# Input normalised with time on the partitions and split once, and the filler ahead of the decay products taken away

## The chip, the cores and the metric

The kernel runs on one core of one Trainium2 chip. The metric is the device time of one execution in microseconds (us), and three executions of a kernel give its median. TensorE (PE) does the matrix products, with a separate queue for its weight loads (PEld); VectorE (DVE), ScalarE (ACT) and GpSimd (POOL) do the elementwise work; SyncE (SP) issues most transfers.

## What is computed

One layer of a hybrid decoder for 1024 time steps and a model width of 1024, all in float32:

```python
xn = rms_norm(x, norm_g)                 # x * rsqrt(mean(x*x, -1) + eps) * g
cols = split_columns(xn @ w_in)
y_a = nsa_attention(cols["a_q"], ...) * silu(cols["a_z"])
y_b = swa_sink_attention(cols["b_q"], ...) * silu(cols["b_z"])
y_c = rwkv7_time_mix(cols["c_shift"], ...) * silu(cols["c_z"])
gates = sigmoid(cols["merge"] + b_merge)
mixed = gates_a * (y_a @ proj_a) + gates_b * (y_b @ proj_b) + gates_c * (y_c @ proj_c)
out = rms_norm(x + mixed @ w_out, final_g)
```

The change is in the first line and in the order of a part of `xn @ w_in`.

## The kernel before

The kernel runs as one program in four parts. `trunk` begins with a prologue that loads x, normalises it and keeps it on the chip as two halves of precision, `x_hi` and `x_lo` (x_hi is x rounded to the shorter type fp32r, x_lo the rest), laid out with the model width on the partitions and time along the row. Then come `rwkv` (branch C, in two passes), `attention` (branches A and B) and `finish` (gates, the three output projections, the last product and the last norm).

Every projection of xn is done by `mm3`: for each of the 8 blocks of 128 along the width, three products, hi by hi, hi by lo and lo by hi. A projection to 128 columns takes 48 matmuls of 128x512, 24 for each half of time, and its weights are loaded and split in the same way by `split_w` (ACT rounds, L196; DVE subtracts, L197). The matmuls of these projections are the rows `pj` (L311, L313, L315).

32 projections (8 gates `z0` to `z7` and 24 merge gates) have no user until late. They are the filler: `fill` is a list of tasks, and `fill.run(ns)` writes so many nanoseconds of their matmuls, by a nominal cost of each, at that place of the program. The budgets are constants (`G_0` ahead of the decay products, `G_LORA` behind them, and so on). What the budgets leave is written by `fill.drain()` when attention has been written. A scheduler that works when the program is built then fixes the order of the rows on each engine, and each engine works through its rows in that order. Each filler task ends with a tanh on ACT, for the z gates a product on DVE (`gs`, L358 and L359), and a store.

The prologue reads the transposed input `xT` in two halves of time (`xr`, 8 blocks of 128x512 each). For each block ACT rounds x times `norm_g` (L235), DVE subtracts (L236), and PE begins the first two projections with it, `wa` (the decay features) and `k0`, on the x that is not yet normalised (L240 to L242). ACT squares the block (L244), DVE and POOL add the squares (L249), and PE sums them over the partitions (L254) and spreads the root over them (L263). DVE then scales the two products by it (L268). After that each block is made once more, now normalised: DVE scales it (L271), ACT rounds (L272), DVE subtracts (L273). The projections `z6` and `z7` follow side by side, all 96 matmuls of them, and then `rwkv` begins.

In `rwkv` the path is serial in its first part: `wa` is evacuated (`z`, L424), shifted in time (POOL L433, DVE L434), goes through a tanh (L438) and into the decay products (L460). From these come exponentials, a scan, the sums over heads (`head_sums`, L400 and L401), and with these the tiles AR and BK, whose products are the first matmuls of the chunks (`GM`, L528). Filler matmuls stand between these steps in PE's order.

At the end `finish` loads the branch outputs `y`, scales and splits them (`y_hi` L1208, `y_lo` L1209) and begins with `pp`, the products of branch C, from y6 and y7.

Of the kernel before, what the change touches and what calls it, by code (L numbers as in the profile page):

```python
# [17 lines left out]
P = 128  # L18
# [24 lines left out]
G_0, WP, PSP = 7200, 1, 0  # L43
START = "wa:0-2 x0:0-1 k0:0-2 x0:1-2 wa:2-8 x0:2-3 k0:2-8 x0:3-4 x0:4-6 x0:6-8 x1:0-2 x1:2-4 x1:4-6 x1:6-8"
# [110 lines left out]
def trunk(ctx, tc, a, out):  # L155
# [46 lines left out]

    x_hi = xhp.tile([P, KT, T], F32R, name="x_hi")
# [3 lines left out]
    first = {}  # L207
    pj0_stack = ExitStack()
    pj0 = pj0_stack.enter_context(tc.tile_pool(name="pj0", bufs=1, space=PSUM))
    with tc.tile_pool(name="x0", bufs=1) as x0, tc.tile_pool(name="x0p", bufs=1, space=PSUM) as x0p:  # L210
        names, xrs = ("wa", "k0"), []
        ws = {n: [x0.tile([P, KT * P], F32R, name=f"w{i}{n}") for i in range(2)] for n in names}
        mean = lined(x0, 1, name="mean")
        dve.memset(mean, 1.0 / D)
        ones = x0.tile([P, P], F32, name="ones")
        pool.memset(ones, 1.0)
        act.activation(lined(x0, 1, name="warm"), eps[:, 0:1], AF.Sqrt)
        for step in START.split():
            what, c = step.split(":")
            c0, c1 = [int(i) for i in c.split("-")]  # L220
            if what in names:
                c = slice(c0 * P, c1 * P)
                load_w(x0.tile([P, (c1 - c0) * P], F32, name=f"raw{step}"), a["w"][W_TILES[what]][:, c], ws[what][0][:, c], ws[what][1][:, c])
            else:
                h = int(what[1])
                if c0 == 0:
                    xrs.append(x0.tile([P, KT, NH], F32, name="xr", bufs=2))
                nc.sync.dma_start(xrs[h][:, c0:c1], a["xT"][:, c0:c1, h * NH:(h + 1) * NH])
        for h in range(2):
            ts = slice(h * NH, (h + 1) * NH)  # L230
# [101 lines left out]
    def side_by_side(*pairs):  # L332

        ws = [weights(name) for name, _ in pairs]
        for h in range(2):
# [3 lines left out]
            for _ in range(KT):  # L339
                for gen in gens:  # L340
                    for _ in range(3):
                        yield next(gen)
# [983 lines left out]
```

## Time and profile before

| | us |
|---|---|
| median of 3 runs | 1198.23 (1197.81 to 1201.52) |
| the profiled execution, its own time | 1200.41 |
| its span, from the first to the last instruction | 1198.6 |
| PE busy in it | 1132.8 (95%) |
| mean granted clock of PE | 0.984 |

The span is the part of an execution that the trace shows. PE's granted clock has two levels, 2.4 GHz (1.00 in a row) and 1.2 GHz; a mean between them says what share of a stretch had which.

### The profile page before, as it was taken

To read this page: it belongs to the slowest core of one execution; us is meant where nothing else is said; L and a number is where in the kernel's file an instruction comes from. 1 tells how busy PE (TensorE), PEld (TensorE's weight loads), DVE (VectorE), ACT (ScalarE), POOL (GpSimd) and SP (SyncE) were. 2 spreads that over 40 slices of the span, in tenths; PEclk is the share of its full clock that TensorE was granted. 3 is DMA by queue.
4 is the path that set the end of the run, shared out by engine and by line. 5 is a ranking of instruction groups with operands and counts; after the bars stand their busy time and mean duration, and the time that the engine had idled before them with its cause. 6 is when DMAs were issued, how large, how long until landed. Compare 5 with 4: busy or idle time off the path is not lost.

```text
span 1198.6 us, 18003 instructions
## 1 busy us (share of the span) xinstructions
PE 1132.8 (95%) x6698; PEld 915.0 (76%) x6698; DVE 769.1 (64%) x1449; ACT 555.9 (46%) x1283; POOL 279.4 (23%) x288
## 2 busy tenths in 40 slices
PE   7698999999999989998999999999999995999997
PEld 5566888767887889886878877887788774778886
DVE  7947782479643632268387878746887776887332
ACT  7435332462423532254466666636666663222322
POOL 3110100021000211127123322231323222263222
PEclk9889999999999999999999999999999998999999
DMA  5121224021231222113111111111211137884221
GB/s 194 35 84 62 62 74 118 28 79 58 66 110 46 62 92 91 31 44 92 59 49 60 60 64 52 50 49 62 63 49 54 40 108 242 298 273 145 71 71 54
DMA packets 66456, 101.92 MB, mean 85 GB/s; under 512 B 16832, under 2 KB 27456, under 8 KB 66112
## 3 DMA queue, kind: packets, MB, share of 16 engines
q1 hardware_dynamic: 64160, 96.41, 25.0%
q10 hardware_dynamic: 1440, 2.26, 0.5%
q0 software_dynamic: 768, 2.10, 0.5%
q8 instruction: 53, 0.87, 0.3%
q14 instruction: 35, 0.29, 0.1%
HBM read 70.86 MB, written 27.79 MB: 82 GB/s over the span
## 4 chain that ended last, share of the span: by engine, by line
PE 71%; DVE 16%; DMA 5%; ACT 4%; issue 2%; POOL 1%; SPq 0%; POOLq 0%; ACTq 0%; DVEq 0%
PE pj L311 12%; PE pj L313 12%; PE pj L315 12%; PE s L1059 4%; PE tr L901 4%; DVE p L1095 3%; PE op L315 2%; PE op L311 2%; PE op L313 2%; PE pv L892 2%; PE pv L893 2%; ACT p L1068 1%; PE pp L311 1%; PE pp L315 1%; PE pp L313 1%
## 5 line engine op out<-in xcount | busy, mean ns | idle before, releaser
L311 PE MATMUL pj<-x_hi,wh 128*128 128x512 f32 x768 | 308.4, 402 | 8.0 <-DVE gs L359 3.7
L315 PE MATMUL pj<-x_hi,wl 128*128 128x512 f32 x768 | 306.0, 399 | 2.7 <-DVE wl L197 2.7
L313 PE MATMUL pj<-x_lo,wh 128*128 128x512 f32 x768 | 306.7, 399 | 0.0
L311 PEld LDWEIGHTS pj<-x_hi,wh 128*128 128x128 f32 x768 | 145.8, 190 | 40.2 <-DVE gs L359 5.1
L315 PEld LDWEIGHTS pj<-x_hi,wl 128*128 128x128 f32 x768 | 145.7, 190 | 31.8 <-DVE wl L197 3.1
L313 PEld LDWEIGHTS pj<-x_lo,wh 128*128 128x128 f32 x768 | 145.8, 190 | 29.3 <-issue 1.3
L196 ACT ACTIVATE wh<-wr 128x512 fp32r<-128x512 f32 (+1 forms) x120 | 70.1, 599 | 114.2 <-PE pj L313 78.6
L1068 ACT ACTIVATE p<-s,nm 128x512 f32<-128x512 f32 (+3 forms) x160 | 93.3, 588 | 50.1 <-DVE nm L1065 30.2
L903 ACT ACTIVATE th<-tr 128x512 fp32r<-128x512 f32 x132 | 78.5, 597 | 56.7 <-PE tr L901 48.0
L905 DVE TENSOR_TENSOR tl<-tr,th 128x512 fp32r<-128x512 f32 x132 | 89.8, 685 | 22.5 <-ACT th L903 19.8
L197 POOL TENSOR_TENSOR wl<-wr,wh 128x512 fp32r<-128x512 f32 x52 | 67.9, 1318 | 151.0 <-ACT wh L196 116.8
L1065 DVE TENSOR_REDUCE nm<-s 128x1 f32<-128x512 f32 (+3 forms) x130 | 85.0, 660 | 20.2 <-PE s L868 17.9
L901 PE MATMUL tr<-ident,p 128*128 128x128 f32 x528 | 81.9, 277 | 12.8 <-DVE tl L905 12.1
L901 PEld LDWEIGHTS tr<-ident,p 128*128 128x128 f32 x528 | 62.2, 141 | 29.2 <-DVE tl L905 15.7
L1059 PE MATMUL s<-k,q 128*128 128x512 f32 (+3 forms) x320 | 82.8, 356 | 0.9 <-ACT p L1068 0.6
L197 DVE TENSOR_TENSOR wl<-wr,wh 128x512 fp32r<-128x512 f32 (+1 forms) x68 | 52.7, 787 | 39.3 <-ACT wh L196 38.9
L892 PE MATMUL pv<-th,V 128*128 128x512 f32 (+1 forms) x162 | 68.3, 427 | 2.0 <-DVE o L873 1.5
L1059 PEld LDWEIGHTS s<-k,q 128*128 128x128 f32 x320 | 53.9, 188 | 16.5 <-ACT p L1068 7.3
L1095 DVE TENSOR_SCALAR p<-p,nm 128x512 f32<-128x512 f32 (+3 forms) x160 | 64.9, 472 | 0.7
L311 PE MATMUL pp<-y_hi,wh 128*128 128x512 f32 x128 | 51.2, 401 | 10.8 <-ACT y_hi L1208 6.9
L893 PE MATMUL pv<-tl,V 128*128 128x512 f32 (+1 forms) x162 | 60.6, 380 | 0.0
L881 POOL TENSOR_TENSOR ol<-ol,o 64x512 f32<-64x512 f32 x16 | 20.9, 1304 | 135.9 <-DMA ol<-o 135.9
(322 smaller groups left out, 2090.6 us busy)
## 6 DMA issues: line engine op xcount, KB each, us to landing
wr<-w SPq DMA_DIRECT2D x96, 256.0 KB, 2.8
g_scr<-gs SPq DMA_DIRECT2D x48, 256.0 KB, 2.0
g<-g_scr SPq DMA_DIRECT2D x24, 512.0 KB, 5.4
z_scr<-gs SPq DMA_DIRECT2D x16, 256.0 KB, 2.2
wor<-w_out SPq DMA_DIRECT2D x8, 512.0 KB, 4.8
x<-x SPq DMA_DIRECT2D x8, 512.0 KB, 5.8
xr<-xT SPq DMA_DIRECT2D x6, 512.0 KB, 9.1
w<-w SPq DMA_DIRECT2D x2, 1024.0 KB, 6.2
```

The costliest lines, as they stand in the source:

```text
L197: weng[0].tensor_sub(lo, raw, hi.bitcast(F32))
L311: pe.matmul(ps, lh, rh, start=k == 0, stop=False)
L313: pe.matmul(ps, lh, rl, start=False, stop=False)
L315: pe.matmul(ps, ll, rh, start=False, stop=k == n - 1)
L892: pe.matmul(pv, v.rearrange("p j d -> p (j d)"), th, start=start, stop=False, skip_group_check=True)
L893: pe.matmul(pv, v.rearrange("p j d -> p (j d)"), tl, start=False, stop=stop, skip_group_check=True)
L901: pe.transpose(tr[:, h], p4[h], ident)
L905: dve.tensor_sub(tl, tr, th.bitcast(F32))
L1059: pe.matmul(ps[:, i], q[h0 + i][:, qs], ks[j][:, kc:kc + n], start=i == 0 and j == 0, stop=wrap and j == 1, skip_group_check=True)
L1065: dve.tensor_reduce(nm[:, c, 0, hs], ps, axis=AX.X, op=OP.max, negate=True)
L1068: act.activation(weights(h, c), ps[:, i], AF.Exp, bias=nm[:, c, 0, h:h + 1], accum_out=nm[:, c, 1, h:h + 1])
L1095: eng.tensor_scalar(p, p, nm[:, c, 3, h:h + 1], None, op0=OP.mult)
```

## The change

x is loaded in 8 blocks of 128 time steps (time on the partitions, 1024 values in each row). ACT squares a block and sums each row in the same instruction (L290), takes the root (L291), and DVE inverts it (L292) and scales the block by its one scalar per row (L293). PE transposes the block in pieces of 128x128 into PSUM, four to a tile `tr` of 128x512 (L298): two blocks of time by two of the width. ACT rounds a half of such a tile times `norm_g` into `x_hi` (128x256, L301) and DVE writes `x_lo` (L302). The first two projections are made of these in pieces of 128x256, for one pair of blocks after the other (`begun`). The second split, the scaling of the products and the sums of squares over the partitions are gone. The weights of z6 are loaded among the first loads; the first half of z6 is written behind the second pair, and the budget `G_0` ahead of the decay products is 0. z7 and the rest of z6 go to the filler as ordinary tasks. `mm3`, `weights`, `product`, `project` and the gates' functions stand further up, unchanged but for an argument `w` of `project` (weights already there); `side_by_side` is gone. Line numbers behind the prologue are 24 lower after the change (L460 becomes L436, L400 L376, L528 L504, L1009 L985), and mm3's matmuls are L214, L216 and L218.

```diff
-G_0, WP, PSP = 7200, 1, 0
-START = "wa:0-2 x0:0-1 k0:0-2 x0:1-2 wa:2-8 x0:2-3 k0:2-8 x0:3-4 x0:4-6 x0:6-8 x1:0-2 x1:2-4 x1:4-6 x1:6-8"
+G_0, WP, PSP = 0, 1, 0
+START = "x:0 wa:0-2 x:1 wa:2-8 k0:0-2 x:2 k0:2-8 x:3 z6 x:4 x:5 x:6 x:7"
...
+    fill = Stream()
+    hvec = lined(cst, NVEC, name="hvec")
+    dve.tensor_scalar(hvec, vec, 0.5, None, op0=OP.mult)
...
-        mean = lined(x0, 1, name="mean")
-        dve.memset(mean, 1.0 / D)
-        ones = x0.tile([P, P], F32, name="ones")
-        pool.memset(ones, 1.0)
         act.activation(lined(x0, 1, name="warm"), eps[:, 0:1], AF.Sqrt)
         for step in START.split():
-            what, c = step.split(":")
-            c0, c1 = [int(i) for i in c.split("-")]
-            if what in names:
+            what, *c = step.split(":")
+            if what == "x":
+                xrs.append(x0.tile([P, D], F32, name="xr", bufs=6))
+                nc.sync.dma_start(xrs[-1], a["x"][len(xrs) * P - P:len(xrs) * P])
+            elif what in names:
+                c0, c1 = [int(i) for i in c[0].split("-")]
                 c = slice(c0 * P, c1 * P)
                 load_w(x0.tile([P, (c1 - c0) * P], F32, name=f"raw{step}"), a["w"][W_TILES[what]][:, c], ws[what][0][:, c], ws[what][1][:, c])
             else:
-                h = int(what[1])
-                if c0 == 0:
-                    xrs.append(x0.tile([P, KT, NH], F32, name="xr", bufs=2))
-                nc.sync.dma_start(xrs[h][:, c0:c1], a["xT"][:, c0:c1, h * NH:(h + 1) * NH])
-        for h in range(2):
-            ts = slice(h * NH, (h + 1) * NH)
-            accs = [None, None]
-            for n in names:
+                w6 = weights(what)
+        for n in names:
+            for h in range(2):
                 first[n, h] = pj0.tile([P, NH], F32, name=f"p{n}{h}")
+
+        def normalised(i):
+            ts = slice(2 * i * P, 2 * i * P + 2 * P)
+            for xr in xrs[2 * i:2 * i + 2]:
+                ss = lined(x0, 2, name="ss", bufs=4)
+                act.activation(x0.tile([P, D], F32, name="sq", bufs=2), xr, AF.Square, accum_out=ss[:, 0:1])
+                act.activation(ss[:, 1:2], ss[:, 0:1], AF.Sqrt, bias=eps[:, 0:1], scale=1.0 / D)
+                dve.reciprocal(ss[:, 1:2], ss[:, 1:2])
+                dve.tensor_scalar(xr, xr, ss[:, 1:2], None, op0=OP.mult)
+            for k2 in range(0, KT, 2):
+                tr = x0p.tile([P, 2, 2, P], F32, name="tr", bufs=2)
+                for j in range(2):
+                    for b in range(2):
+                        pe.transpose(tr[:, j, b], xrs[2 * i + b][:, (k2 + j) * P:(k2 + j + 1) * P], ident)
+                for j in range(2):
+                    k, t = k2 + j, tr[:, j].rearrange("p b t -> p (b t)")
+                    act.activation(x_hi[:, k, ts], t, AF.Copy, scale=col("norm_g", k))
+                    dve.scalar_tensor_tensor(x_lo[:, k, ts], t, col("norm_g", k), x_hi[:, k, ts].bitcast(F32),
+                                             op0=OP.mult, op1=OP.subtract)
+
+        def begun(i):
+            h, o = divmod(i, 2)
+            ts = slice(2 * i * P, 2 * i * P + 2 * P)
             for k in range(KT):
-                act.activation(x_hi[:, k, ts], xrs[h][:, k], AF.Copy, scale=col("norm_g", k))
-                dve.scalar_tensor_tensor(x_lo[:, k, ts], xrs[h][:, k], col("norm_g", k), x_hi[:, k, ts].bitcast(F32),
-                                         op0=OP.mult, op1=OP.subtract)
                 for n in names:
+                    ps = first[n, h][:, 2 * o * P:2 * o * P + 2 * P]
                     hi, lo = [w[:, k * P:(k + 1) * P] for w in ws[n]]
-                    pe.matmul(first[n, h], hi, x_hi[:, k, ts], start=k == 0, stop=False)
-                    pe.matmul(first[n, h], lo, x_hi[:, k, ts], start=False, stop=False)
-                    pe.matmul(first[n, h], hi, x_lo[:, k, ts], start=False, stop=k == KT - 1)
-                sq = x0.tile([P, NH], F32, name="sq", bufs=4)
-                act.activation(sq, xrs[h][:, k], AF.Square)
-                j = k % 2
-                if k < 2:
-                    accs[j] = sq
-                else:
-                    (dve if j else pool).tensor_add(accs[j], accs[j], sq)
-            dve.tensor_add(accs[0], accs[0], accs[1])
-
-            ss = x0p.tile([P, NH], F32, name="ss", bufs=2)
-            for j in range(4):
-                pe.matmul(ss[:, j:j + 1], accs[0][:, j * P:(j + 1) * P], mean, start=True, stop=True,
-                          skip_group_check=True)
-            rq = lined(x0, 4, name="rq", bufs=2)
-            act.activation(rq, ss[:, 0:4], AF.Sqrt, bias=eps[:, 0:1])
-            dve.reciprocal(rq, rq)
-            diag = x0.tile([P, 4, P], F32, name="diag")
-            dve.tensor_tensor(diag, ident.unsqueeze(1).to_broadcast([P, 4, P]), rq.unsqueeze(2).to_broadcast([P, 4, P]),
-                              op=OP.mult)
-            ss = x0p.tile([P, NH], F32, name="ss", bufs=2)
-            pe.matmul(ss, ones, diag.rearrange("p j t -> p (j t)"), start=True, stop=True)
-            rms = x0.tile([P, NH], F32, name="rms", bufs=2)
-            act.activation(rms, ss, AF.Copy)
-
-            for n in names:
-                dve.tensor_mul(first[n, h], first[n, h], rms)
-            for k in range(KT):
-                xn = xrs[h][:, k]
-                dve.scalar_tensor_tensor(xn, xn, col("norm_g", k), rms, op0=OP.mult, op1=OP.mult)
-                act.activation(x_hi[:, k, ts], xn, AF.Copy)
-                dve.tensor_sub(x_lo[:, k, ts], xn, x_hi[:, k, ts].bitcast(F32))
+                    pe.matmul(ps, hi, x_hi[:, k, ts], start=k == 0, stop=False, skip_group_check=True)
+                    pe.matmul(ps, lo, x_hi[:, k, ts], start=False, stop=False, skip_group_check=True)
+                    pe.matmul(ps, hi, x_lo[:, k, ts], start=False, stop=k == KT - 1, skip_group_check=True)
+
+        fill.add(project(*zgate(6), w6))
+        normalised(0)
+        for i in range(4):
+            if i < 3:
+                normalised(i + 1)
+            begun(i)
+            if i == 1:
+                fill.run(5000)
...
-    fill = Stream()
-    pair = side_by_side(zgate(6), zgate(7))
-    fill.add(pair)
-    fill.need(pair)
-    fill.add(*[project(*zgate(i)) for i in (4, 5, 0, 1, 2, 3)])
+    fill.add(*[project(*zgate(i)) for i in (7, 4, 5, 0, 1, 2, 3)])
```

Where the order of PE moves, at three places. At the start of the program PE began before with the first products, on blocks of 512 time steps (`pwa` and `pk` are the accumulators of wa and k0, `w0` and `w1` the hi and lo weights):

```order
L240 MATMUL pwa_133<-x_hi,w0wa 128x512
L241 MATMUL pwa_133<-x_hi,w1wa 128x512
L242 MATMUL pwa_133<-x_lo,w0wa 128x512
L240 MATMUL pk_134<-x_hi,w0k_97 128x512
L241 MATMUL pk_134<-x_hi,w1k_98 128x512
L242 MATMUL pk_134<-x_lo,w0k_97 128x512
```

Now it begins with eight transposes, two tiles of four, and later transposes stand between the products of 256 time steps:

```order
L298 MATMUL tr<-ident,xr 128x128 x8
L312 MATMUL pwa_163<-x_hi,w0wa 128x256
L313 MATMUL pwa_163<-x_hi,w1wa 128x256
L314 MATMUL pwa_163<-x_lo,w0wa 128x256
L312 MATMUL pk_165<-x_hi,w0k_117 128x256
L313 MATMUL pk_165<-x_hi,w1k_118 128x256
L314 MATMUL pk_165<-x_lo,w0k_117 128x256
L312 MATMUL pwa_163<-x_hi,w0wa 128x256
L313 MATMUL pwa_163<-x_hi,w1wa 128x256
L312 MATMUL pk_165<-x_hi,w0k_117 128x256
L313 MATMUL pk_165<-x_hi,w1k_118 128x256
L298 MATMUL tr<-ident,xr 128x128 x4
```

The transposes are the rows that came in, 16 of four in all; each product is now cut in two (192 matmuls of 128x256 for 96 of 128x512), and the products with `x_lo` of a block can stand behind the next transposes.

At the decay products (L460 before, L436 now; `pj` is the filler), before, around the second half of them:

```order
L313 MATMUL pj<-x_lo,wh 128x512
L315 MATMUL pj<-x_hi,wl 128x512
L311 MATMUL pj<-x_hi,wh 128x512
L460 MATMUL g<-wa,wa_591 128x512 x2
L313 MATMUL pj<-x_lo,wh 128x512
L315 MATMUL pj<-x_hi,wl 128x512
L311 MATMUL pj<-x_hi,wh 128x512
```

Now, around all four:

```order
L216 MATMUL pj<-x_lo,wh 128x512
L218 MATMUL pj<-x_hi,wl 128x512
L214 MATMUL pj<-x_hi,wh 128x512
L436 MATMUL g<-wa,wa_620 128x512 x4
L216 MATMUL pj<-x_lo,wh 128x512
L218 MATMUL pj<-x_hi,wl 128x512
L214 MATMUL pj<-x_hi,wh 128x512
```

Before, 96 pj matmuls stood ahead of the first two decay products and 130 ahead of the second two; now 46 stand ahead of all four (24 of them among the first products, 22 right ahead). At the first head sum the count was 164 and is 78, at the first matmul of GM 288 and 192; from there through rwkv and attention it stays lower by two tasks (96 matmuls, at one step 97).

At the end of attention, before, the last product of attention (L1009) and the first products of finish (`pp`):

```order
L892 MATMUL pv<-th,V 128x512
L893 MATMUL pv<-tl,V 128x512
L892 MATMUL pv<-th,V 128x512
L893 MATMUL pv<-tl,V 128x512
L1009 MATMUL pv<-th,vcc 128x512
L311 MATMUL pp<-y_hi,wh 128x512
L313 MATMUL pp<-y_lo,wh 128x512
L315 MATMUL pp<-y_hi,wl 128x512
```

Now, around the same product (L985):

```order
L868 MATMUL pv<-th,V 128x512
L869 MATMUL pv<-tl,V 128x512
L868 MATMUL pv<-th,V 128x512
L869 MATMUL pv<-tl,V 128x512
L985 MATMUL pv<-th,vcc 128x512
L216 MATMUL pj<-x_lo,wh 128x512
L218 MATMUL pj<-x_hi,wl 128x512
L214 MATMUL pj<-x_hi,wh 128x512
L216 MATMUL pj<-x_lo,wh 128x512
```

Before, the last pj matmul stands ahead of L1009 with 33 other rows between, and pp follows L1009 at once. Now 28 pj matmuls more stand among the last blocks of attention, and 68 follow L985 without a break; pp comes behind them.

## Rows read from the trace of the kernel before

**Rows 1.** Windows: us; busy of PE, PEld, DVE, ACT, POOL; PE clock, DMA share, GB/s.

```profile
0.00:130.00 130.00, 107.62 (x418) 81.70 (x418) 94.17 (x117) 66.97 (x106) 26.15 (x43) 0.92 0.26 87
130.00:984.75 854.75, 834.33 (x5432) 678.71 (x5432) 551.15 (x1143) 424.68 (x1039) 182.54 (x189) 1.00 0.21 64
97.71:129.93 32.22, 31.46 (x128) 24.92 (x129) 24.84 (x24) 13.68 (x18) 1.99 (x2) 0.95 0.17 53
984.75:1002.60 17.85, 12.31 (x60) 8.56 (x58) 15.36 (x29) 8.97 (x23) 6.99 (x8) 0.90 0.85 282
1002.60:1013.93 11.33, 3.51 (x14) 2.36 (x14) 4.48 (x8) 2.57 (x6) 3.17 (x3) 0.84 0.56 171
```

**Rows 2.** Timeline of PE: start us, us, row, [idle before <- releaser].

```profile
5.14 0.80 PE L240 MATMUL pwa<-x_hi,w0wa 128*128 128x512 f32 x1 [5.14 <-ACT x_hi L235]
85.40 1.13 PE L460 MATMUL g<-wa,wa 64*128 64x512 f32 x4
97.71 0.50 PE L400 MATMUL g<-hi,blk 128*128 128x512 f32 x1 [3.23 <-ACT hi L490]
129.93 1.16 PE L528 MATMUL g<-AR,BK 64*128 64x128 f32 x16
```

**Rows 3.** Waits of PE: two of the prologue: total us, times, longest us.

```profile
PE pwa L242 <- DVE x_lo L236: 5.1, 2, 4.9
PE pj L311 <- DVE gs L359: 3.7, 1, 3.7
```

**Rows 4.** Timelines of PE and POOL: end of attention, start of finish.

```profile
1002.60 0.51 PE L1009 MATMUL pv<-th,vcc 128*128 128x512 f32 x1 [0.42 <-DVE th L1006]
1013.93 1.22 PE L311 MATMUL pp<-y_hi,wh 128*128 128x512 f32 x2 [6.89 <-ACT y_hi L1208]
1017.08 0.44 PE L313 MATMUL pp<-y_lo,wh 128*128 128x512 f32 x1
1010.49 0.67 POOL L883 DMA_DIRECT2D oa_scr<-ol  x1 [0.29 <-POOL ol L882]
```

**Rows 5.** Transfers of the first 60 us: GB/s in slices of 1.5 us.

```profile
GB/s 0 174 267 211 269 367 398 406 389 386 389 388 184 36 0 0 0 0 0 16 0 0 5 0 0 0 0 0 0 0 59 173 117 168 160 22 0 0 0 0
```

**Rows 6.** Single durations, timelines of ACT and DVE.

```profile
95.58 1.04 ACT L486 ACTIVATE sq<-kk 128x1024 f32<-128x1024 f32 x1
1182.43 0.29 ACT L1275 ACTIVATE ss<-ss,eps 128x1 f32<-128x1 f32 x1 [0.23 <-DVE ss L1273]
87.29 0.70 DVE L464 TENSOR_SCALAR lora<-lora 128x1024 f32<-128x1024 f32 x1 [2.62 <-ACT lora L463]
```

**Rows 7.** Timeline of PE: matmuls at half clock, at full clock, and 256 wide.

```profile
9.57 0.63 PE L241 MATMUL pk<-x_hi,w1k 128*128 128x512 f32 x1
10.00 0.51 PE L242 MATMUL pk<-x_lo,w0k 128*128 128x512 f32 x1
505.12 0.39 PE L311 MATMUL pj<-x_hi,wh 128*128 128x512 f32 x1
505.80 0.39 PE L311 MATMUL pj<-x_hi,wh 128*128 128x512 f32 x1
1186.11 0.28 PE L313 MATMUL op<-o_lo,mh 128*128 128x256 f32 x1
1186.59 0.28 PE L315 MATMUL op<-o_hi,ml 128*128 128x256 f32 x1
```

**Rows 8.** Timeline of PE: four transposes and the row behind; the page: all of them.

```profile
987.29 0.60 PE L901 MATMUL tr<-ident,p 128*128 128x128 f32 x4
987.64 0.48 PE L893 MATMUL pv<-tl,V 128*128 128x512 f32 x1
L901 PE MATMUL tr<-ident,p 128*128 128x128 f32 x528 | 81.9, 277 | 12.8 <-DVE tl L905 12.1
```

**Rows 9.** Durations by line: ns min/median/max, first and last start.

```profile
L986 ACT ACTIVATE p<-s x16: 377/385/401, 595.3 to 983.3; 128x256 f32<-128x256 f32 x16
L987 DVE TENSOR_TENSOR p<-p,s x16: 408/418/423, 596.7 to 985.2; 128x256 f32<-128x256 f32 x16
```

More of the change, by code (lines that the diff above doesn't have):

```diff
@@ L322, in product, with project @@
         return mm3(ps, lambda k: (hi[:, k], lo[:, k]), lambda k: (x_hi[:, k, ts], x_lo[:, k, ts]), KT)
-    def project(name, evac):
-        hi, lo = weights(name)
+    def project(name, evac, w=None):
+        hi, lo = w or weights(name)
         for h in range(2):
@@ L330, in project @@
             evac(h, ts, ps)
-    def side_by_side(*pairs):
-        ws = [weights(name) for name, _ in pairs]
-        for h in range(2):
-            ts = slice(h * NH, (h + 1) * NH)
-            pss = [pj.tile([P, NH], F32, name="pj") for _ in pairs]
-            gens = [product(*w, ts, ps) for w, ps in zip(ws, pss)]
[L339 to L342, printed above, removed]
-            for gen, (_, evac), ps in zip(gens, pairs, pss):
-                dense(gen)
-                evac(h, ts, ps)
     y_scr = tc.dram_tile([2, P, T], F32, name="y_scr")
@@ L373, in trunk @@
     fill = Stream()
-    pair = side_by_side(zgate(6), zgate(7))
-    fill.add(pair)
-    fill.need(pair)
-    fill.add(*[project(*zgate(i)) for i in (4, 5, 0, 1, 2, 3)])
+    hvec = lined(cst, NVEC, name="hvec")
+    dve.tensor_scalar(hvec, vec, 0.5, None, op0=OP.mult)
+    first = {}
+    pj0_stack = ExitStack()
+    pj0 = pj0_stack.enter_context(tc.tile_pool(name="pj0", bufs=1, space=PSUM))
+    with tc.tile_pool(name="x0", bufs=1) as x0, tc.tile_pool(name="x0p", bufs=1, space=PSUM) as x0p:
+        names, xrs = ("wa", "k0"), []
+        ws = {n: [x0.tile([P, KT * P], F32R, name=f"w{i}{n}") for i in range(2)] for n in names}
+        act.activation(lined(x0, 1, name="warm"), eps[:, 0:1], AF.Sqrt)
+        for step in START.split():
+            what, *c = step.split(":")
[4 more added lines that the diff above has]
+                c0, c1 = [int(i) for i in c[0].split("-")]
+                c = slice(c0 * P, c1 * P)
+                load_w(x0.tile([P, (c1 - c0) * P], F32, name=f"raw{step}"), a["w"][W_TILES[what]][:, c], ws[what][0][:, c], ws[what][1][:, c])
+            else:
+                w6 = weights(what)
+        for n in names:
+            for h in range(2):
+                first[n, h] = pj0.tile([P, NH], F32, name=f"p{n}{h}")
+        def normalised(i):
[19 more added lines that the diff above has]
+            ts = slice(2 * i * P, 2 * i * P + 2 * P)
+            for k in range(KT):
+                for n in names:
+                    ps = first[n, h][:, 2 * o * P:2 * o * P + 2 * P]
+                    hi, lo = [w[:, k * P:(k + 1) * P] for w in ws[n]]
+                    pe.matmul(ps, hi, x_hi[:, k, ts], start=k == 0, stop=False, skip_group_check=True)
[9 more added lines that the diff above has]
+                fill.run(5000)
@@ new lines, in trunk @@
+    identb = cst.tile([P, P], BF16, name="identb")
+    pool.tensor_copy(identb, ident)
+    blk1 = cst.tile([P, P], F32R, name="blk1")
+    with tc.tile_pool(name="blk", bufs=1) as bp:
+        blk0 = bp.tile([P, P], F32, name="blk0")
+        pool.memset(blk0, 0.0)
+        pool.memset(blk0[0:64, 0:64], 1.0)
+        pool.memset(blk0[64:128, 64:128], 1.0)
+        pool.tensor_copy(blk1, blk0)
+    caus = cst.tile([P, P], BF16, name="caus")
+    pool.memset(caus, 0.0)
+    pool.affine_select(caus, caus, pattern=[[-1, P]], compare_op=OP.is_ge, fill=NEG, base=0,
+                       channel_multiplier=1)
@@ new lines, in trunk @@
+    cmpm = cst.tile([P, NB, 64], BF16, name="cmpm")
+    pool.memset(cmpm, 0.0)
+    pool.affine_select(cmpm, cmpm, pattern=[[P, NB], [-16, 64]], compare_op=OP.is_ge, fill=NEG, base=-31,
+                       channel_multiplier=1)
+    seen = cst.tile([P, P], F32, name="seen")
+    pool.memset(seen, 1.0)
+    pool.affine_select(seen, seen, pattern=[[-1, P]], compare_op=OP.is_ge, fill=0.0, base=0, channel_multiplier=1)
+    seen = seen.bitcast(mybir.dt.uint32)
+    pool.memset(rowok, 1.0)
+    pool.affine_select(rowok, rowok, pattern=[[0, 1]], compare_op=OP.is_ge, fill=0.0, base=-31,
+                       channel_multiplier=1)
```

41 lines of the change are left out of this document (removed).

## The prediction

> **What bounds the kernel now.** I read the windows first, which give PE's busy time by stage. From 130 to 985 us PE is busy for 834 of 855 us at full clock [rows 1]: that long middle is bound by PE's work, and a matmul added there or taken away counts in full. The first 130 us are different: PE is busy for 107.6 us only, at a mean granted clock of 0.92. So are the end of attention (12.3 of 17.9 us, clock 0.90) and the start of finish (3.5 of 11.3 us, clock 0.84) [rows 1]. Then I read the timeline of PE for the steps of the serial path: first product at 5.14, second half of the decay products at 85.40, first head sum at 97.71, first matmul of GM at 129.93 [rows 2]. Last come the waits: in the prologue PE stands for 4.9 us for a first `x_lo` and for 3.7 us for the evacuation of a z gate [rows 3]. The reader is to see that time can come out only at the two ends, and that filler taken from the front has to be run somewhere else.
>
> **The front, part by part.** The x of before must arrive 8 blocks deep for a half; now two blocks of 128 rows do (with the first weights between them 1.18 MB). The transfers of before had moved that much by about 6.7 us (slices of 0.26, 0.40, 0.32, 0.40 MB from 1.5 to 7.5 us) [rows 5]. Behind it stand a square of 128x1024 (1.04, a row with no sum, as the nearest), a root (0.29), an inverse (taken as long as the root, 0.29) and a product by a scalar (0.70) [rows 6], 2.3 us in all, and some 0.6 for the hand-overs between engines (the root waited 0.23 for its input). The first transposes start at 9.6, 4.5 us later than PE starts now.
>
> From there PE's work up to the decay products is counted from the order. It has 192 matmuls of 128x256 at 0.12 (1186.11 to 1186.59 for four), 23.0 us; 46 of 128x512 at 0.227 (505.12 to 505.80 for three), 10.4 us [rows 7]; and 64 transposes. Four of these and the hand-over to the next row take 0.35 us [rows 8], 0.09 each, 5.8 us. Sum 39.2. Now PE runs at half clock (0.43 for 128x512) from its start to 10.0 [rows 2, 7], which costs 4.86 x 0.47 = 2.3; I charge the same again. Stalls: nothing at least, 4.9 at most as the longest of before; I take 2. The decay products then begin at 9.6 + 39.2 + 2.3 + 2.0 = 53.1.
>
> This holds if ACT and DVE keep up. ACT has 32 roundings of 128x256 from PSUM at about 0.39, DVE as many subtractions at 0.42 [rows 9], 12.5 and 13.4 us, with 8 squares with roots (10.6) on the one, 8 products with inverses (7.9) on the other [rows 6], and the weight splits, which are the same as before but for those of z7, which move away. That is 23 and 21 us beside 39 of PE. The removed second split was on DVE's path: it is the reason for the 4.9 us above.
>
> Before, the second half of the decay products stood at 85.40; now all four are together, so the second half is 1.1 later than the first (a pair takes 1.13 [rows 2]), at 54.2. From it to the first head sum 12.3 us pass now, by exponentials and a scan on ACT, DVE and POOL with no lack of filler on PE; I keep them: 66.5. From there to GM it is 32.2 us, PE busy for 31.5 and DVE for 24.8 [rows 1]. In that stretch the order has 114 filler matmuls for 124, 10 x 0.227 = 2.3 less, if DVE's chain lets it (0 otherwise): 30.0, and GM at 96.5. **The front gives 129.9 - 96.5 = 33.4 us.** The budget of 7200 ns is in this, and the 96 matmuls of z6 and z7 less the 46 that stay.
>
> **The middle.** From GM to the end of attention the order of filler is one of the same task phases, two tasks behind. PE has the same matmuls there; nothing changes.
>
> **The end.** 96 filler matmuls (21.8 us) arrive here. 28 of them, 6.4 us, stand among the last attention blocks, where PE has 5.5 us idle and lost another 1.8 to the clock (0.10 of 17.9), while DVE is busy for 15.4 us [rows 1]. I take them as free; the bound is 6.4. The other 68 stand behind the last attention product: 15.4 us. Before, pp comes there: 12 products from y6, and then a wait of 6.9 until y7 is ready 11.33 us behind the last attention product (1002.60 to 1013.93). This wait goes back to the store of the last attention block (1010.49), whose memory y7's tile reuses [rows 4]. The chain to that store has no filler in it, so it runs under the 68 matmuls. PE passes the same point after 0.3 + 15.4 + 12 x 0.227 = 18.4 us in place of 11.3, +7.1. Without its stall PE need not restart at half clock, as it does now from 1013.93 to 1017.08 [rows 4], which costs 3.15 x 0.47 = 1.5. **The end costs 7.1 - 1.5 = 5.6 us.** The weights of the first output projection use the buffers of the last filler tasks but one; those of the second wait for the last filler matmul, with 24 pp matmuls (5.4 us) to hide it.
>
> **Sum.** -33.4 + 5.6 = -27.8 us. The profiled span of 1198.6 becomes 1170.8; the profiled execution took 1200.41, 2.2 above the median, so on the median 1198.23 - 27.8 = 1170.4. As a check by waste alone: PE's lost time in the front (22.4 idle, and 0.08 x 130 = 10.4 of clock) falls to about 9.6 + 2.3 + 2 + 3.2 (the wait ahead of the head sum [rows 2]) = 17, some 16 less; at the end 5.5 + 7.8 idle and 3.6 of clock [rows 1] go nearly to nothing, some 14 to 16 less; the transposes (5.8) and the narrow products (23.0 for 96 x 0.227 = 21.8) add 7. That gives -23 to -25, and more by what the removed sums of squares took on PE, which I leave out: if anything, the sum by the path is on the low side.
>
> **A price in dispute.** The four transposes take 0.35 us with their hand-over, but the row of all of them has a mean of 277 ns each [rows 8], which is from start to end. I take the row of four, as the spacing is what PE's path pays; by the mean the 64 would cost 17.7 in place of 5.8, and that is rival D. The Trainium skill ("TensorE: Matmul & The Clock Gate", Part 4: PE-mode transpose) gives about 275 ns for one in a kernel. By that figure the 64 would come to 17.6 us, an estimate from the page; the trace's mean agrees with the figure, its spacing doesn't.
>
> **Rivals.**
> A, the forecast, 1170.4: 55%. Its own range goes from 1162 to 1180: the stalls (0 to 4.9), the 28 at the end (0 to 6.4), the 2.3 before GM, and a start up to 3 us off.
> B, the end doesn't hide. If a transfer or a conversion that pp needs waits for the last filler task (its evacuation on ACT stands ahead of y_hi there, or a buffer is freed by it), the 11.33 us chain comes behind the filler, and all of the 21.8 us is paid: -33.4 + 21.8 = -11.6, 1186.6. Against it: y7 is held by attention's store only in what I see. 12%.
> C, slower. PE waits at each of 16 tiles of transposes for evictions through two buffers, and stays at half clock through the whole prologue. Of 39.2 us of work 2.3 is counted already, so 36.9 more: +9.1, 1207.3. It decides against the change when 30 of the 39 us (77%) are at half clock. For it: behind its wait of 5.14 PE is at half clock until 10.0 [rows 2, 7], and the new prologue has a longer one. Against it: the end of attention, with waits at the same kind of tiles, shows 0.90 [rows 1]. 7%.
> D, the transposes are paid at 277 ns each without overlap: 64 x (0.277 - 0.09) = 12.0 more, 1182.4. Against it the row of four. 8%.
> E, better: no stall, clock up from the start (-4.3), and the rest of the waste at the end gone too (-3): 1163. 13%.
> F, nothing is left: two of B, C and D in part. 5%.
>
> A measurement of this kernel tells about 0.3%, 3.6 us, from no change. Faster by more: A, B, D, E, 0.88. Within: F, 0.05. Slower: C, 0.07. For the range A, most of E and B are needed: 1159 to 1188.
>
> **What would show it.** In the profile of the changed kernel: first transpose near 9.6, decay products near 53, first head sum near 66, first matmul of GM near 97, with transposes 0.09 apart at full clock; from GM to the last attention product a stretch as long as before; then 68 filler matmuls without a gap and no wait of PE for y_hi. A wait for y_hi behind the filler is B, a prologue with a clock well below 0.8 is C, transposes 0.28 apart are D. The forecast is wrong if the middle does not keep its length, that is if filler that arrives later leaves gaps in PE there.

## The result and the profile after

The change makes the kernel faster by 1.7%: 1178.33 us (1177.64 to 1179.98) for 1198.82 (1197.81 to 1201.52), a ratio of 0.9828 (95% interval 0.9808 to 0.9848), that is 20.5 us (18.2 to 23.0). The forecast was -27.8 us, with the right sign and a third too large. The front came out as forecast, to the tenth; the end did not.

The windows of the changed kernel, cut at the first matmul of GM, the last attention product but one, the last one, and the pp products behind the y7 chain (columns as in [rows 1]):

```profile
0.00:96.51 96.51, 82.20 (x461) 69.71 (x461) 62.05 (x92) 53.28 (x101) 16.29 (x36) 1.00 0.29 100
96.51:948.70 852.19, 835.16 (x5424) 681.26 (x5424) 544.82 (x1140) 425.34 (x1036) 186.64 (x191) 0.99 0.20 63
948.70:972.05 23.35, 18.61 (x98) 14.22 (x96) 19.86 (x33) 11.24 (x28) 10.89 (x10) 1.00 0.77 259
972.05:992.07 20.02, 20.02 (x81) 16.45 (x82) 10.74 (x18) 9.64 (x19) 3.23 (x3) 0.92 0.63 194
992.07:1176.00 183.93, 173.58 (x781) 142.72 (x779) 92.11 (x149) 49.00 (x105) 60.74 (x45) 0.99 0.45 154
```

The timeline of PE at the steps that [rows 2] and [rows 4] show of before:

```profile
7.56 0.45 PE L298 MATMUL tr<-ident,xr 128*128 128x128 f32 x1 [7.56 <-DVE xr L293]
8.85 1.76 PE L298 MATMUL tr<-ident,xr 128*128 128x128 f32 x7 [0.84 <-DVE xr L293]
...
11.21 0.42 PE L312 MATMUL pk<-x_hi,w0k 128*128 128x256 f32 x1
11.43 0.42 PE L313 MATMUL pk<-x_hi,w1k 128*128 128x256 f32 x1
...
16.42 0.28 PE L312 MATMUL pk<-x_hi,w0k 128*128 128x256 f32 x1
16.54 0.28 PE L313 MATMUL pk<-x_hi,w1k 128*128 128x256 f32 x1
...
55.18 1.99 PE L436 MATMUL g<-wa,wa 64*128 64x512 f32 x8 [1.33 <-ACT z L400]
...
68.30 0.50 PE L376 MATMUL g<-hi,blk 128*128 128x512 f32 x1 [1.18 <-ACT hi L466]
...
96.51 1.16 PE L504 MATMUL g<-AR,BK 64*128 64x128 f32 x16
...
972.05 0.79 PE L985 MATMUL pv<-th,vcc 128*128 128x512 f32 x1 [2.51 <-DVE th L982]
972.64 0.63 PE L216 MATMUL pj<-x_lo,wh 128*128 128x512 f32 x1
973.07 0.63 PE L218 MATMUL pj<-x_hi,wl 128*128 128x512 f32 x1
...
989.35 0.39 PE L214 MATMUL pp<-y_hi,wh 128*128 128x512 f32 x1
...
992.07 0.39 PE L214 MATMUL pp<-y_hi,wh 128*128 128x512 f32 x1
```

GM begins at 96.51 for 129.93, 33.4 us earlier. From there to the last attention product it takes 875.5 us for 872.7 (129.93 to 1002.60), 2.9 longer. From that product to the pp products behind the y7 chain (992.07, no wait before it) it takes 20.0 for 11.33, 8.7 longer, and the rest of finish 183.9 for 184.7. So the end costs 10.8 us, and -33.4 + 10.8 = -22.6 is the difference of the two spans, 1176.0 and 1198.6. (The medians differ by 2.1 us less: the profiled execution of before, 1200.41, is 1.6 us above the median 1198.82, and that of the change 0.5 below its own.) The rows also show the new wait: the last attention product stands for 2.51 us, for a split on DVE (`th`, L982), and the filler behind it runs at half clock (0.43 from 972.64 to 973.07).

What DVE did there, in its own timeline, and the row of ACT that the second split waits for:

```profile
968.53 0.38 ACT L981 ACTIVATE th<-tr 64x256 fp32r<-64x256 f32 x1 [1.48 <-DVE th L982]
...
970.84 0.69 DVE L1183 TENSOR_TENSOR y<-y,z 128x512 f32<-128x512 f32 x1 [2.35 <-DMA z<-z_scr]
971.57 0.43 DVE L982 TENSOR_TENSOR th<-tr,th 64x256 fp32r<-64x256 f32 x1
```

The split at 971.57 was ready to run from 968.9, when ACT had written its half of `th`; ahead of it in DVE's order stands a product of finish, y5 with its gate (L1183), which waits 2.35 us for its load.

### The profile page after: what moved, and what is told of

Its sections match the earlier page's. It is cut to its first block, busy times and chain, and to the rows that moved or that the text cites. A ratio compares the mean times of both kernels' runs of the same rounds, so it can differ in the third digit from the quotient of the medians.

```text
span 1176.0 us, 18273 instructions
## 1 busy us (share of the span) xinstructions
PE 1129.6 (96%) x6838; PEld 924.4 (79%) x6838; DVE 729.6 (62%) x1428; ACT 548.5 (47%) x1287; POOL 277.8 (24%) x285
## 3 DMA queue, kind: packets, MB, share of 16 engines
q10 hardware_dynamic: 1440, 2.26, 0.5%
## 4 chain that ended last, share of the span: by engine, by line
PE 73%; DVE 13%; ACT 4%; DMA 4%; issue 2%; POOL 2%; SPq 0%; POOLq 0%; DVEq 0%; ACTq 0%
PE pj L214 12%; PE pj L218 12%; PE pj L216 12%; PE s L1035 4%; PE tr L877 3%; DVE p L1071 3%; PE op L218 2%; PE op L216 2%; PE op L214 2%; PE pv L869 2%; PE pv L868 2%; PE pp L214 2%; PE pp L218 2%; PE pp L216 2%; ACT p L1044 1%
## 5 line engine op out<-in xcount | busy, mean ns | idle before, releaser
L214 PE MATMUL pj<-x_hi,wh 128*128 128x512 f32 x768 | 307.7, 401 | 3.5 <-DVE gs L247 2.8
L218 PE MATMUL pj<-x_hi,wl 128*128 128x512 f32 x768 | 305.9, 398 | 0.0
L216 PE MATMUL pj<-x_lo,wh 128*128 128x512 f32 x768 | 305.4, 398 | 0.0
L214 PEld LDWEIGHTS pj<-x_hi,wh 128*128 128x128 f32 x768 | 145.6, 190 | 35.1 <-DVE gs L247 3.6
L216 PEld LDWEIGHTS pj<-x_lo,wh 128*128 128x128 f32 x768 | 145.7, 190 | 28.8 <-issue 1.1
L218 PEld LDWEIGHTS pj<-x_hi,wl 128*128 128x128 f32 x768 | 145.5, 190 | 28.7
L197 POOL TENSOR_TENSOR wl<-wr,wh 128x512 fp32r<-128x512 f32 x56 | 73.6, 1326 | 149.8 <-ACT wh L196 109.8
L881 DVE TENSOR_TENSOR tl<-tr,th 128x512 fp32r<-128x512 f32 x132 | 89.5, 684 | 24.0 <-ACT th L879 21.6
L197 DVE TENSOR_TENSOR wl<-wr,wh 128x512 fp32r<-128x512 f32 (+1 forms) x64 | 49.3, 784 | 36.3 <-ACT wh L196 36.1
L214 PE MATMUL pp<-y_hi,wh 128*128 128x512 f32 x128 | 50.4, 393 | 3.8 <-DVE mixed L1222 2.3
L1227 POOL TENSOR_TENSOR mixed<-mixed,t 128x512 f32<-128x512 f32 x28 | 39.2, 1425 | 53.8 <-DVE t L1225 53.8
```

What stands on the lines that cost most here:

```text
L197: weng[0].tensor_sub(lo, raw, hi.bitcast(F32))
L214: pe.matmul(ps, lh, rh, start=k == 0, stop=False)
L216: pe.matmul(ps, lh, rl, start=False, stop=False)
L218: pe.matmul(ps, ll, rh, start=False, stop=k == n - 1)
L881: dve.tensor_sub(tl, tr, th.bitcast(F32))
```

## The experiments

Ratios are to the kernel before, timed on the same chip in the same rounds, with 95% intervals.

| kernel | ratio | interval |
|---|---|---|
| the change | 0.9828 | 0.9808 to 0.9848 |
| the change again | 0.9826 | 0.9805 to 0.9847 |
| new prologue alone | 0.9925 | 0.9911 to 0.9940 |
| filler moved alone, 144 matmuls | 1.0035 | 1.0023 to 1.0047 |
| filler moved alone, 96 matmuls | 0.9954 | 0.9939 to 0.9969 |
| transposes twice | 0.9895 | 0.9883 to 0.9908 |
| six buffers in finish | 0.9846 | 0.9832 to 0.9860 |
| gate products on POOL | 0.9826 | 0.9803 to 0.9849 |
| 47 filler matmuls behind, for 68 | 0.9788 | 0.9771 to 0.9806 |
| the same, gate products on POOL | 0.9803 | 0.9781 to 0.9824 |
| 28 behind | 0.9790 | 0.9773 to 0.9806 |
| 2 behind | 0.9821 | 0.9805 to 0.9837 |

**The change again.** The changed kernel itself, to compare three others with it.

> The changed kernel itself once more, to compare the next three with it on one chip: 0.983 of the kernel before, 1178.

It gave 0.9826. Its profile shows the same end: the last attention product waits 3.69 us for DVE, and the last block, the stretch to the pp products behind the y7 chain and the rest take 24.5, 20.9 and 181.6 us for 20.1, 11.3 and 184.7 before, 10.9 more in sum (10.8 in the first profile).

**The prologue and the filler apart.** First the new prologue with the filler where it stood before:

```diff
-G_0, WP, PSP = 0, 1, 0
+G_0, WP, PSP = 7200, 1, 0
...
-    fill.add(*[project(*zgate(i)) for i in (7, 4, 5, 0, 1, 2, 3)])
+    ahead = project(*zgate(7))
+    fill.add(ahead)
+    fill.need(ahead)
+    fill.add(*[project(*zgate(i)) for i in (4, 5, 0, 1, 2, 3)])
```

> The new prologue alone: z6 and z7 are finished ahead of the decay products and the budget of 7200 is back, so that filler stands where it stood before the change (163 matmuls ahead of the first head sum, 164 before). Theory: the change has two halves, the prologue itself and 96 filler matmuls (21.8 us) that go from the front, where PE was full, to the end, where the changed kernel pays 10.8 us for them. Then the first matmul of GM stands at 96.5 + 21.8 = 118, the end is that of the kernel before, and the time is 1198.8 - 11.6 = 1187. Rival 1, the move of the filler only shifts a cost: the time stays at that of the changed kernel, 1178. Rival 2, the prologue gains nothing by itself: 1199.

It gave 0.9925, 9.0 us less than before, where 11.6 were expected. Its timeline of PE has the place and the end that the theory gave:

```profile
73.42 1.99 PE L439 MATMUL g<-wa,wa 64*128 64x512 f32 x8
...
118.80 1.16 PE L507 MATMUL g<-AR,BK 64*128 64x128 f32 x16
...
1004.81 0.79 PE L214 MATMUL pp<-y_hi,wh 128*128 128x512 f32 x1 [5.75 <-ACT y_hi L1187]
```

GM stands at 118.80 (118 expected), and behind the last attention product the wait for y7 is there again, 5.75 us. Both rivals fall. The other half, the old prologue with the filler moved, was run in two sizes. With 144 matmuls moved:

```diff
-G_0, WP, PSP = 7200, 1, 0
+G_0, WP, PSP = 0, 1, 0
...
-    pair = side_by_side(zgate(6), zgate(7))
-    fill.add(pair)
-    fill.need(pair)
-    fill.add(*[project(*zgate(i)) for i in (4, 5, 0, 1, 2, 3)])
+    fill.add(*[project(*zgate(i)) for i in (6, 7, 4, 5, 0, 1, 2, 3)])
```

> The old prologue with z6 and z7 as ordinary filler and no budget ahead of the decay products: 94 filler matmuls ahead of the first head sum for 164, and 144 (32.7 us) later from there on. Theory: the decay path then waits for DVE, whose second split runs to 64 us, so the decay products begin at about 68 and GM at 112, 18 us earlier for 32.7 us of work moved; the end pays some 20; about 1201, no gain. Rival: taking the filler away from the front is what gains, with either prologue: 11 us, 1188.

It gave 1.0035: slower by 4 us, as the theory had it (1201 for some 1203). With z6 left ahead, so that 96 are moved as in the change (the lines that differ from the diff above):

```diff
+    ahead = project(*zgate(6))
+    fill.add(ahead)
+    fill.need(ahead)
+    fill.add(*[project(*zgate(i)) for i in (7, 4, 5, 0, 1, 2, 3)])
```

> The old prologue with z6 whole ahead of the decay products, z7 as ordinary filler and no budget ahead of the decay products, so that from GM on the filler stands as in the changed kernel (96 later than before, 68 behind the last attention product). Theory: the decay path waits for DVE's second split, the decay products stand at 67 as with 144 moved, GM at 110, 20 us earlier than before, and the end costs 10.8 as in the changed kernel: 9 us less than before, 1190. Rival, filler taken from the front gains nothing with the old prologue: 1199 to 1203.

It gave 0.9954, 5.5 us less than before, where 9 were expected; the rival (nothing) falls too. Its timeline of PE, and that of DVE at the end of the second split:

```profile
68.10 1.99 PE L460 MATMUL g<-wa,wa 64*128 64x512 f32 x8 [0.15 <-ACT z L424]
...
108.30 1.16 PE L528 MATMUL g<-AR,BK 64*128 64x128 f32 x16
...
990.12 0.39 PE L1009 MATMUL pv<-th,vcc 128*128 128x512 f32 x1
...
1008.29 0.39 PE L311 MATMUL pp<-y_hi,wh 128*128 128x512 f32 x1
```

```profile
61.64 1.88 DVE L273 TENSOR_TENSOR x_lo<-xr,x_hi 128x512 fp32r<-128x512 f32 x3
64.70 1.28 DVE L434 SCALAR_TENSOR_TENSOR wa<-d,vec,z 128x1024 f32<-128x1024 f32 x1 [0.58 <-POOL blk L283]
```

DVE writes the last `x_lo` of the second split until 63.5 and only then shifts `wa` (64.70); the decay products follow at 68.10. From the last attention product to the pp products behind the y7 chain it takes 18.2 us (990.12 to 1008.29): the forecast's 18.4, without a wait and at full clock. What is missing to the expected 9 lies between GM and the last attention product (881.8 us for 872.7). Of these 9.1 us, 3.3 are in the last block of attention (23.4 for 20.14), as in the changed kernel (3.2), though the last product doesn't wait here: there are 3.1 us of waits for other splits, and the granted clock is 0.93. The other 5.9 are in the long middle before it, where the kernel with the new prologue alone loses 2.3 too (854.8 for 852.5); with the filler moved alone:

```profile
108.30:966.71 858.41, 838.09 (x5422) 681.21 (x5421) 546.03 (x1141) 426.38 (x1036) 189.81 (x191) 0.99 0.20 64
...
411.24:417.45 6.21, 6.21 (x18) 5.78 (x19) 4.00 (x4) 2.66 (x3) 0.00 (x0) 0.50 0.25 98
```

Here PE runs at half clock for 6.2 us from 411.24 and for another 3.1 from 615.57, where it kept full clock in the profile of the kernel before; half of these 9.3 us is most of the 5.9. Whether that belongs to the kernel or to the one execution that was profiled is not shown.

So the halves don't add in the whole: 9.0 and 5.5 apart, 20.5 together. At the step that both are about they nearly do: GM comes 11.1 us earlier with the new prologue alone (118.80), 21.6 with the filler moved alone (108.30), 32.7 in sum, and 33.4 with both. The decay products stand at 85.40 (second half) before, at 73.42 with the new prologue alone, at 68.10 with the filler moved alone, at 55.18 with both. With the filler kept PE's work ahead of them sets the time (no wait), with the old prologue DVE's second split does. What is missing in the sum of the halves stands in the long middle of their two profiles (2.3 and 5.9), not there.

**The price of the transposes.**

```diff
-                for j in range(2):
+                for j in (0, 1, 0, 1):
                     for b in range(2):
                         pe.transpose(tr[:, j, b], xrs[2 * i + b][:, (k2 + j) * P:(k2 + j + 1) * P], ident)
```

> The changed kernel with each of the 64 transposes done twice into the same place. Theory (0.09 us each by spacing): at most 5.8 us more, some of it in PE's waits: 1181 to 1184. Rival (0.277 us each, by the mean duration): 17.7 more, 1196. Rival (hidden in the waits for evictions): 1178.

It gave 0.9895, 8.1 us more than the change, where at most 5.8 were expected. PE's timeline:

```profile
18.64 1.04 PE L298 MATMUL tr<-ident,xr 128*128 128x128 f32 x8
19.43 0.36 PE L314 MATMUL pk<-x_lo,w0k 128*128 128x256 f32 x1
...
62.27 1.99 PE L436 MATMUL g<-wa,wa 64*128 64x512 f32 x8 [1.33 <-ACT z L400]
...
75.39 0.79 PE L376 MATMUL g<-hi,blk 128*128 128x512 f32 x1 [1.13 <-ACT hi L466]
...
105.93 1.16 PE L504 MATMUL g<-AR,BK 64*128 64x128 f32 x16
```

Eight transposes and the hand-over take 0.79 us (18.64 to 19.43), 0.10 each, and the decay products come 7.1 us later for 64 of them (62.27 for 55.18), 0.11 each, the first of them at half clock. From there to GM another 2.3 us are lost (105.93 for 96.51 is 9.4), since PE falls to half clock behind the wait ahead of the head sum (75.39, 0.79 for a 128x512), which it did not in the change. The spacing is the price, not the duration of 277 ns in [rows 8]: rival D falls, and so does "hidden".

**The wait of the last attention product.** With one more buffer the scheduler puts the gate's product behind the split:

```diff
-    HB_, GB, YB, TT_, OB = 5, 4, 14, 3, 1
+    HB_, GB, YB, TT_, OB = 6, 4, 14, 3, 1
```

> The changed kernel with six buffers in place of five for the rows of width 1024 in finish (HB_), so that the products of y5 with its gate no longer stand ahead of the last split of attention (th, L982) in DVE's order. Theory: the wait of 2.5 us of the last attention product goes, and with it the half clock behind it (1.6): 1178.3 - 4 = 1174. Rival: that product waits for the attention's own chain: 1178.

PE's timeline shows that the theory holds for the place, and that the time is lost again:

```profile
966.66 0.40 PE L985 MATMUL pv<-th,vcc 128*128 128x512 f32 x1
...
982.35 0.39 PE L214 MATMUL pp<-y_hi,wh 128*128 128x512 f32 x1
...
988.95 0.47 PE L214 MATMUL pp<-y_hi,wh 128*128 128x512 f32 x1 [1.00 <-ACT wh L196]
```

The last product has no wait, there is no half clock, and pp begins at 982.35 for 989.35. But finish then waits for its weights again and again (1.00 us at 988.95, then 0.74 and 0.93): on SP the loads of y6 and y7 now wait for the last attention product itself, they go out at 967 for 947 in the change, the loads of y4 and y5 queued behind them are late, and the weights come no earlier than in the change (990.4 for 990.8). From the first pp to the end it takes 198.5 us for 186.7. The whole is 0.9846, no better than the change. A cleaner way leaves the buffers alone:

```diff
-                        dve.tensor_mul(y[:, ts], y[:, ts], z[:, ts])
+                        pool.tensor_mul(y[:, ts], y[:, ts], z[:, ts])
```

> The changed kernel with the products of y4 and y5 with their gates (L1183) on POOL and no longer on DVE, where one of them stood ahead of the last split of attention and waited for its load. Theory: the last attention product no longer waits (2.5 us), PE does not fall to half clock behind it (1.6), pp starts 4 us earlier and finish keeps its length: 4 us less than the changed kernel. Rival: what is won at pp is given back in finish, whose transfers have a share of 0.86 there, as with six buffers: no difference.

The rival is right: 0.9826. PE's timeline:

```profile
950.53 0.48 PE L985 MATMUL pv<-th,vcc 128*128 128x512 f32 x1
...
971.43 0.50 PE L985 MATMUL pv<-th,vcc 128*128 128x512 f32 x1
...
987.19 0.39 PE L214 MATMUL pp<-y_hi,wh 128*128 128x512 f32 x1
...
994.55 0.47 PE L214 MATMUL pp<-y_hi,wh 128*128 128x512 f32 x1 [1.76 <-DVE mixed L1222]
...
1000.27 0.50 PE L214 MATMUL pp<-y_hi,wh 128*128 128x512 f32 x1 [2.29 <-DVE mixed L1222]
```

From the last product but one to the first pp it takes 36.7 us (950.53 to 987.19) for 40.7 in the change, so the 4 us are won there. Then pp waits 1.76 and 2.29 us for its evacuations (`mixed`), which stand in DVE's order behind the splits of the y tiles, and from the first pp to the end it takes 191.4 us for 186.7. The wait was real, but finish's own start was ready no earlier: it was later, by this edit. SP and ACT in this run, and behind them in the change:

```profile
975.56 0.32 SPq L1173 DMA_DIRECT2D y<-oa_scr  x1
975.99 0.48 SPq L855 DMA_DIRECT2D ol<-o  x1
986.11 2.19 ACT L1184 ACTIVATE y_hi<-y 128x512 fp32r<-128x512 f32 x4 [8.39 <-DMA oa_scr<-ol]
...
973.60 0.48 SPq L855 DMA_DIRECT2D ol<-o  x1
983.28 2.19 ACT L1184 ACTIVATE y_hi<-y 128x512 fp32r<-128x512 f32 x4 [3.39 <-DMA oa_scr<-ol]
```

The splits wait for the store of attention's last block (`oa_scr`), and this store begins with the copy `ol<-o` on SP. Ahead of that copy stands a load of finish (L1173), which waits 2.6 us for the product on POOL. So the copy goes out 4.6 us behind the last attention product, in the change 1.6, and the first `y_hi` behind the store begins 14.7 us after that product for 11.2. The run takes away one wait and puts in another, and does not show what the first is worth alone.

**How much filler belongs behind.** The budget of the last blocks of attention was raised, which takes filler from behind the last attention product to ahead of it:

```diff
-G_Q, G_SCORE, G_OWN, G_FIRST, G_LAST = (1510, 90, 1110), (500, 950, 950), 390, (780, 1390, 1330), (480, 1140, 700)
+G_Q, G_SCORE, G_OWN, G_FIRST, G_LAST = (1510, 90, 1110), (500, 950, 950), 390, (780, 1390, 1330), (480, 1140, 1150)
```

> The changed kernel with a larger budget in the last blocks of attention (1150 for 700), which brings 21 of the 68 filler matmuls behind the last attention product ahead of it (47 stay, 10.7 us, and with 12 pp products 13.4 us, still over the 11.3 of the y7 chain). Theory: PE stands idle for 4.7 us of the last attention block and pays 18.4 us for a chain of 11.3 behind it, so up to 4.8 us come out: 3 to 5 less than the changed kernel. Rival: the last block is set by its loads and DVE's order, and the filler put there delays it by as much as it saves behind: no difference.

It gave 0.9788, some 4.6 us less than the change; the two intervals just touch. The windows, cut as above:

```profile
948.22:973.12 24.90, 22.94 (x119) 18.48 (x118) 20.60 (x34) 12.57 (x30) 9.80 (x10) 1.00 0.76 266
973.12:987.44 14.32, 14.10 (x61) 11.18 (x60) 3.84 (x7) 4.52 (x10) 3.23 (x3) 1.00 0.43 134
```

The last block of attention takes 24.9 us for 23.35 with 21 matmuls (4.8 us) more in it, PE busy for 22.9, without the wait and at full clock; behind it 14.3 for 20.0. The two together take 39.2 us, for 43.4 and 45.4 in the two profiles of the change. The series goes on with 28 and 2 behind (budgets 1550 and 2100 in the same line):

> The changed kernel with the budget of the last blocks of attention at 1550 for 700: 28 filler matmuls (6.4 us) stay behind the last attention product, with 12 pp products 9.1 us, less than the 11.3 of the y7 chain. Theory: 40 matmuls (9.1 us) more stand inside, where 4.7 us were idle, so the attention's last product comes some 4 later than in the changed kernel; behind it PE has to wait for y7 again, some 2 us; the time lies between the changed kernel and the one with 47 behind: 0.979 to 0.983 of the kernel before. Rival, the fewer behind the better: under 0.979.

> The same with the budget at 2100: 2 filler matmuls stay behind the last attention product. Theory: the wait for y7 is open again, 11.3 - 3.2 = 8 us, with the half clock behind it, while the attention's last product comes about 10 later than in the changed kernel: pp goes on 1 to 3 us later than in the changed kernel, 0.983 to 0.986 of the kernel before. Rival, the place of the filler makes no difference as PE's work is the same: 0.983 and 0.979 would then be noise, and this one 0.981.

They gave 0.9790 and 0.9821. The waits of y7 in the timelines of PE, with 28 behind and with 2:

```profile
989.17 0.73 PE L214 MATMUL pp<-y_hi,wh 128*128 128x512 f32 x2 [1.18 <-ACT y_hi L1184]
```

```profile
996.98 0.79 PE L214 MATMUL pp<-y_hi,wh 128*128 128x512 f32 x1 [6.86 <-ACT y_hi L1184]
```

With 28 a wait of 1.18 us opens, with 2 one of 6.86, and the first pp products behind the latter run at half clock. The ratio with 2 is better than the theory's range (0.983 to 0.986), and its interval takes in the rival's 0.981 too; what speaks against the rival is that 47 and 28 lie together near 0.979 and 68 and 2 near 0.982, and the waits in the rows. So the place does matter, and the best lies between: the filler that about covers the 11 us of the y7 chain. Last, both at once:

```diff
-G_Q, G_SCORE, G_OWN, G_FIRST, G_LAST = (1510, 90, 1110), (500, 950, 950), 390, (780, 1390, 1330), (480, 1140, 700)
+G_Q, G_SCORE, G_OWN, G_FIRST, G_LAST = (1510, 90, 1110), (500, 950, 950), 390, (780, 1390, 1330), (480, 1140, 1150)
...
-                        dve.tensor_mul(y[:, ts], y[:, ts], z[:, ts])
+                        pool.tensor_mul(y[:, ts], y[:, ts], z[:, ts])
```

> 47 filler matmuls behind (budget 1150) and the products of y4 and y5 with their gates on POOL. Theory: with 47 behind the last attention product no longer waits, so POOL has nothing left to take away: as with 47 behind alone, 0.979. Rival: both add, 0.976.

It gave 0.9803, within the interval of 47 behind alone; they don't add.

## Why the prediction was right, and what was off

**The front** was forecast at -33.4 and measured at -33.4, but by terms that made up for each other. The first transpose ran at 7.56 and the rest of the first tiles at 8.85, not 9.6: the first block needn't wait for the second. Half clock held from 8.85 to about 16.2 (0.22 for a 128x256, then 0.12), 7.3 us for the 4.9 taken from before, so 3.4 lost for 2.3. (The granted clock of the window to 96.51 is printed as 1.00; here the spacing of the matmuls is what shows the lower level.) PE had its work ahead of the decay products done at 53.7 (forecast 53.1), but these began at 55.18, after a wait of 1.33 us for the serial chain of `wa`, which I had not priced behind the last product. Against that the stretch from the head sum to GM took 28.2 for the forecast 30.0, which had the 10 matmuls fewer in it already: the clock was 1.00 where it was 0.95 [rows 1], 1.6 of 32.2 us, which the forecast had left as it was. The price of a transpose, 0.09, is 0.10 to 0.11.

**The middle** kept its length as forecast: GM to the last attention product but one takes 852.2 us for 852.5 (129.93 to 982.46).

**The end** is the step that failed, by its size: 5.6 forecast, 10.8 measured. Rival B did not happen, y7 was ready and pp never waited for it. Three terms were too small. "I take them as free" was said of the 28 filler matmuls among the last attention blocks; the last block took 3.2 us more (23.35 for 20.14), where the last product waits 2.5 us behind DVE's product, for 0.4 before. "Without its stall PE need not restart at half clock" missed that the stall had moved: PE restarts at half clock behind the new wait, and the 18.4 forecast became 20.0. (With the filler moved alone, where that wait is absent, the same stretch takes 18.2.) And finish gained 0.7 where 1.5 were forecast. That is 3.2 + 1.6 + 0.8 = 5.6, and -0.3 from the middle. In the prediction's words, DVE was read as busy for 15.4 of 17.9 us there; what counts was not its share but what stands in its order ahead of the split, and what that waits for.

That the wait caused what stands behind it is shown (from the last attention product but one to the first pp it takes 4.0 and 5.8 us less in the POOL run and in the one with six buffers, which are without it); that the kernel would be 4 us faster without it is not, as both edits make finish late by another way. The run with 47 behind shows what is worth having: the surplus of filler (18.4 us behind, for a chain of 11.3) put into PE's gaps in the last block, whose idle time falls from 4.7 us to 2.0, that wait with it. Finish's start is held by the store of attention's last block and by DVE's order of splits behind it, which both show in its rows; how much each holds was not separated.

C (half clock through the prologue), E and F did not happen; D is refuted by the doubled transposes. Of the gain, the new prologue by itself is worth 9.0 us and the moved filler 5.5. The remaining 6 appear only with both, and their cause is open: at GM, behind the step that two different engines held, the two parts add to within 0.7 us.

## What to carry to other kernels

Work that fills gaps is worth what the gaps are: before filler is moved to another place, count the idle time there against the work that arrives, and leave just as much behind the last serial chain as it needs for cover; here 28 to 47 matmuls were better than 68 or 2. When a step is held by two engines in turn, the parts of a change are to be compared at a landmark right behind that step as well as in the whole: here they add at the landmark (32.7 of 33.4 us) and not in the whole (14.5 of 20.5), so what is missing has to be looked for elsewhere. And an engine's order is to be read at the place where another engine waits for it: a row pulled forward that waits for a load holds everything behind it, whatever the engine's share of busy time.

## What the runs showed that was not expected

The long middle, the same instructions from the first matmul of GM to the last attention product but one, took 852.2 us in the first profile of the changed kernel and 849.7 in the second, and 854.4 in the run with 47 behind and the products on POOL, where PE has the same matmuls in that stretch. Such a spread, 2.5 us for one and the same kernel and 4.7 in all, is as large as the smaller effects here, so that single profiles tell such effects only by the stretch in which they arise, and the ratios by their intervals.

The rows show where it comes from. Behind one and the same wait PE keeps full clock in one execution and falls to half in another; the changed kernel in its first and its second profile:

```profile
397.33 0.64 PE L214 MATMUL pjv<-hi,x_hi 128*128 128x408 f32 x2 [2.82 <-ACT hi L762]
396.50:402.50 6.00, 5.17 (x19) 4.90 (x20) 4.02 (x4) 3.44 (x4) 0.00 (x0) 0.72 0.39 154
...
397.48 0.64 PE L214 MATMUL pjv<-hi,x_hi 128*128 128x408 f32 x2 [2.82 <-ACT hi L762]
396.65:402.65 6.00, 5.17 (x26) 4.79 (x27) 4.01 (x4) 3.44 (x4) 0.00 (x0) 1.00 0.43 164
```

In the first PE runs at half clock for some 3 us behind this wait (19 matmuls in the 6 us for 26), and again behind one of 2.26 us at 596.70; in the second behind neither. Each time the rows behind come 1.4 us later, and the two make up the difference of the two profiles there. The third run, with 854.4, has both; its further 2.2 us are not accounted for.
